# Input handed over twice, token-major and feature-major: the first layer starts without transposes

## The chip, the cores and the metric

One NeuronCore of a Trainium2 chip runs the whole program. Its engines are TensorE (PE, with its weight loads as PEld), VectorE (DVE), ScalarE (ACT), GpSimd (POOL) and SyncE (SP), which here only issues transfers. The metric is the device time of one launch in microseconds (us), lower is better.

## The reference, cut to what matters

Two decoder layers over 256 tokens of 1024 features, all in float32. Each layer:

```
u = RMSNorm(h) * g_mix
proj = u @ w_in                     # index q/k/w and ka, va | qb | kb | vb | qa | gate_a | gate_b
mixer A: index scores -> the 64 best causal keys of each query -> attention over them (8 heads)
mixer B: two causal softmax maps for each of 4 heads, their difference weighted by lambda, RMSNorm
h += (sigmoid(gate_a) * (A @ w_branch_a) + sigmoid(gate_b) * (B @ w_branch_b)) @ w_out
h += convffn(RMSNorm(h));  h += sigmoid(RMSNorm(h) @ w_ple_gate) * (p[i] @ w_ple_proj)
```

The norm divides each token by the root of the mean of its squares. This factor 1/rms is one number per token, so the kernel multiplies it onto the projection's result instead of onto its input.

## The kernel before, in words

**Products.** Every operand is split into two fp32r parts, hi and lo (`HL` for activations, `wh` and `wl` for weights), and a product is three matmuls: hi with `wh`, hi with `wl`, lo with `wh` (L335 to L337). In `gemm_a` (L318) a projection of 512 columns has 8 steps, one for each 128 features (k). A step does the three matmuls for both halves of the tokens, so 6 matmuls, and a projection has 48. The result stands in two of four rotating accumulators (`ps_acc`, L117), which `evict` empties after the last step. The activation must stand feature-major (features on the partitions), so token-major `h` is transposed by PE first (`split_T2`, L286: transposes at L298, hi part on ACT at L301, lo part on DVE at L302).

**Weights.** They come in chunks of 512 KB (128 x 1024), each good for two steps. `dma_next` issues the load on SP's queue in order into one of five raw buffers; the split of a chunk is one ACT copy (`wh`, L159) and one DVE subtraction (`wl`, L166), and the subtraction frees the raw buffer and issues the next load. The first two chunks are split by halves (`split_piece`, L172).

**Side work and its order.** The order of every engine's instructions is written out when the program is made. Class `Side` (L59) keeps planned clocks for PE, DVE and ACT. Attention, rope, the selection of keys and the like are threads of stages. After every two steps `tick` (L82) lets each thread emit its next stage if three things hold: its last stage is planned to be done, the planned DVE clock is at most 3.5 us (`LIMIT_US`) ahead of the planned PE clock, and no more than 2 us of side work went onto PE in this tick. After it, one more chunk is split as a rule. Lower priority numbers go first: rows and heads 0, mixers 1, selection of keys (`select_side`) 2. Where a result is needed, `until` (L101) emits side stages alone, with no product between them, until its flag is set: for mixer B before its branch product (L747), for mixer A before its own (L754).

**The start (layer 0).** SP loads `h` in two pieces of 256 columns with chunks 0 and 1 behind each, then the other 512 columns, chunks 2 and 3, the tables, chunk 4 and on. PE does seven warm-up products, transposes k = 0 and 1, two more warm-ups, transposes k = 2 and 3, and begins the index projection (452 columns, chunks 0 to 3). Before its third step `mid` transposes k = 4 to 7; before its seventh step `norm` sums the squares of `h` on ACT (`sq_half`), forms 1/rms on POOL (`rstd`) and starts the thread `th` that makes the rope tables; the index result is evicted with 1/rms as its scale, and its rows (`index_side`) are spawned. Then come the projections qb, kb, vb, qa (8 steps each), four gate products, branch B (two products of 4 steps), branch A (the same) and the rest of the layer.

Of the kernel before, what the change touches and what calls it, by code (L numbers as in the profile page):

```python
# [38 lines left out]
N_WARM = (7, 2)  # L39
# [9 lines left out]
T_AT = 1  # L49
# [10 lines left out]
class Side:  # L60
    """Side work emitted in stages between groups of the main products.

    A thread is a generator; after each stage it yields estimates of the time (us) the stage takes
    on the tensor, vector and scalar engines. A stage is emitted once the tensor engine is expected
    to reach it no earlier than the thread's previous stage ends, so that it is not held up."""
# [43 lines left out]
def decoder_kernel(ctx: ExitStack, tc: tile.TileContext, x, pT, ws, fc, tb, gf, rope, out):  # L109
# [26 lines left out]
    def warm_up(n):  # L136
        """Products without use that keep the tensor engine's clock up while the first loads run."""
        for _ in range(n):
            nc.tensor.matmul(wps, warm[:, :P], warm[:, :512], start=True, stop=True)
    warm_up(N_WARM[0])  # L140

# [1 line left out]
    raws, parts = {}, {}  # L143
    nx = {"dma": 0, "hi": 0, "lo": 0, "cur": 0, "held": 0}

    def dma_next(step=CW):
        l, c = divmod(nx["dma"], NCHUNK)
        raw = wpool.tile([P, CW], F32, name="raw", bufs=RAWS)
        for a in range(0, CW, step):
            nc.sync.dma_start(raw[:, a:a + step], ws[l, c][:, a:a + step])  # L150
        raws[nx["dma"]] = raw
        nx["dma"] += 1

# [18 lines left out]
    def split_piece(a, n):  # L172
        """Columns a to a + n of the next chunk."""
        if a == 0:
            parts[nx["hi"]] = (wpool.tile([P, CW], F32R, name="wh", bufs=SPLITS),
                               wpool.tile([P, CW], F32R, name="wl", bufs=SPLITS))
        raw, (wh, wl) = raws[nx["hi"]], parts[nx["hi"]]
        nc.scalar.activation(wh[:, a:a + n], raw[:, a:a + n], AF.Copy)
        nc.vector.tensor_sub(wl[:, a:a + n], raw[:, a:a + n], wh[:, a:a + n].bitcast(F32))
        if a + n == CW:  # L180
            raws.pop(nx["lo"])
            nx["hi"] += 1
            nx["lo"] += 1
            dma_next()

    def prepare(n_lo, n_hi):
        """Have the parts of the chunks before n_lo and n_hi emitted."""
        while nx["lo"] < min(n_lo, NALL):
            if nx["hi"] == nx["lo"]:
                split_hi()  # L190
            split_lo()
        while nx["hi"] < min(n_hi, NALL):
            split_hi()
# [22 lines left out]

    for c in range(2):
        nc.sync.dma_start(h[:, :, c * 256:(c + 1) * 256], xv[:, :, c * 256:(c + 1) * 256])
        dma_next(512)
    nc.sync.dma_start(h[:, :, HALF[1]], xv[:, :, HALF[1]])  # L220
# [8 lines left out]

    for c in range(RAWS - 2):  # L230
        dma_next()
        if c == T_AT:
            load_tables()
# [19 lines left out]
    def sq_half(ss, hf, tiles=(0, 1)):  # L253
        """ss[hf][:, i] = sum of h^2 / D over half of the columns."""
        for i in tiles:
            junk = sm.tile([P, 512], F32, name="junk", **T2)
            nc.scalar.activation(junk, h[:, i, HALF[hf]], AF.Square, scale=1.0 / 32, accum_out=ss[hf][:, i:i + 1])  # L257
# [15 lines left out]
    class HL:  # L273
        """fp32r parts hi + lo of [128, 8, 256] operands, stored by halves of the k index."""
# [11 lines left out]
    def split_T2(srcs, hf, k0, scale, x, between=None):  # L286
        """Parts (columns k0, k0 + 1 of half hf of x) of the transpose of two [128, 512] tiles; the scale is
        one for all k or a function of k."""
        hi, lo = x.h[hf][:, k0:k0 + 2, :], x.l[hf][:, k0:k0 + 2, :]
        n = 1 if callable(scale) else 2  # L290
        pts = []
        for a in range(0, 2, n):
            pt = ps_tp.tile([P, 2, L], F32, name="tp")[:, :n, :]
            pts.append(pt)
            for j in range(n):
                for i in range(2):
                    c = (k0 + a + j) * P
                    nc.tensor.transpose(pt[:, j, i * P:(i + 1) * P], srcs[i][:, c:c + P], ident)  # L298
        for a in range(0, 2, n):
            s = scale if n == 2 else scale(4 * hf + k0 + a)  # L300
            nc.scalar.activation(hi[:, a:a + n, :], pts[a], AF.Copy, scale=s)  # L301
            nc.vector.scalar_tensor_tensor(lo[:, a:a + n, :], pts[a], s, hi[:, a:a + n, :].bitcast(F32),  # L302
                                           op0=ALU.mult, op1=ALU.subtract)
            if between:
                between(a)
# [12 lines left out]
    def gemm_a(x, ks, weights, n, evict, mid=None, before_evict=None, outer=0):  # L318
        """Token-major product: evict(i, psum) for the two token tiles; mid[s]() before step s. The last
        `outer` k go through the first token tile, then through the second."""  # L320
# [27 lines left out]
    def tables(l, t):  # L348
        """Tables of the layer: rope with gains, lambda, sub-norm gain."""
# [30 lines left out]
    def rope_rows(dst, src, n, tabs, i, dup=False):  # L380
        """dst, src [128, n, 64]"""
        m1 = sm.tile([P, 8, 64], F32, name="m1", **T2)[:, :n, :]
        m2 = sm.tile([P, 8, 64], F32, name="m2", **T2)[:, :n, :]
        tA = tabs[:, i, 0, :].unsqueeze(1)
        nc.vector.tensor_mul(m1, src, tA.broadcast_to([P, n, 64]))
        for a, b in ((0, 32), (32, 0)):
            tB = tabs[:, i, 1, a:a + 32].unsqueeze(1)
            nc.vector.tensor_mul(m2[:, :, a:a + 32], src[:, :, b:b + 32], tB.broadcast_to([P, n, 32]))
        if dup:
            nc.vector.tensor_add(dst, m1.broadcast_to([P, 2, 64]), m2.broadcast_to([P, 2, 64]))  # L390
        else:
            nc.vector.tensor_add(dst, m1, m2)
# [8 lines left out]
    def transposed(srcs, nb, dst):  # L401
        """dst [128, nb, 256] from two token-major [128, nb*128] tiles."""
# [9 lines left out]
    def stacked(q3):  # L412
        """fp32r [128 t, n, 2, 64] of [128 t, n, 64]: the two parts of each head side by side."""
# [6 lines left out]
    def transposed_parts(srcs, dsts):  # L420
        """[128, n, 256] (in tiles of 4) from two stacked [128 t, n, 128]."""
# [12 lines left out]
    def begin(k0):  # L434
        split_T2([h[:, i, HALF[0]] for i in range(2)], 0, k0, lambda k: g0[:, k:k + 1], u,
                 lambda j: split_piece(j * 512, 512))
    begin(0)
    warm_up(N_WARM[1])
    begin(2)
    env, th = tables(0, tbs[0])  # L440

    for l in range(DEPTH):
# [7 lines left out]
        st = {}  # L450

        def mid():
            for k0 in (0, 2):
                split_T2([h[:, i, HALF[1]] for i in range(2)], 1, k0, lambda k: g_mix[:, k:k + 1], u)
                if l == 0:
                    prepare(3 + k0 // 2, 3 + k0 // 2)
            if l:
                norm()
# [3 lines left out]

        def norm():
            if l == 0:
                side.dve += BEHIND_US
                side.spawn(th, 0)
                sq_half(ss, 0)
# [5 lines left out]
        def project(c0, n, name, mid=None):  # L473
            pr = [sm.tile([P, 512], F32, name=f"pr{name}", **T2) for _ in range(2)]

            def ev(i, acc):
                nc.scalar.activation(pr[i][:, :n], acc[:, :n], AF.Copy, scale=st["rs"][:, i:i + 1])
# [85 lines left out]
        def heads_side(pr, nm, is_q):  # L563
            """Rope of eight heads, transposed; 1/rms beside the queries, in the keys."""
# [28 lines left out]
        def maps(qn, product, i, hq, mk):  # L593
            """Four masked score maps, exp'd, [128 t, 4, S]; head 4 hq + 2 m + r."""
# [21 lines left out]
        def ptrans(src, nh, i):  # L616
            """[128 s, nh * blocks, 128 t] of [128 t, nh, S]."""
# [103 lines left out]

# [1 line left out]
        pi = project(C_IDX, N_IDX, "i", {MID_N: mid} if l else {MID_0: mid, 6: norm, 7: more})  # L723
        side.spawn(index_side(pi), 0)
        side.spawn(heads_side(project(C_QB, 512, "q"), "qb", True), 0)
# [50 lines left out]
        def ev_n(i, acc):  # L776
            """Second half of the columns of a token tile, then its norm for the ffn."""
# [175 lines left out]
def _layout(np, inp):  # L953
    """Inputs as the launch reads them: rows and columns moved, nothing computed."""
# [47 lines left out]
    return {"x": inp["x"][0], "pT": pT, "ws": ws, "fc": np.stack(fc), "tb": np.stack(tb), "gf": np.stack(gf), "rope": rope}  # L1002
# [19 lines left out]
```

## Time and profile before

| | |
|---|---|
| Time, median of 3 runs | 800.34 us (798.68 to 802.0) |
| Span of the profiled execution | 798.6 us, 0.1 us below the fastest of the three runs |
| Busy share of the span | PE 99%, PEld 86%, DVE 76%, ACT 60%, POOL 8% |
| Chain that ended last | PE 93%, DVE 2%, POOL, ACT, DMA and issue 1% each |
| Granted TensorE clock | full in the records from early in the span to its end |
| Index, qb, kb projections begin (PE) | 7.91, 18.84, 29.7 us |

The span runs from the first to the last instruction. The profile gives no separate device time for the profiled execution, so its own time is taken as its span.

### The profile page before, as it was taken

To read this page: it belongs to the slowest core of one execution; us is meant where nothing else is said; L and a number is where in the kernel's file an instruction comes from. 1 tells how busy PE (TensorE), PEld (TensorE's weight loads), DVE (VectorE), ACT (ScalarE), POOL (GpSimd) and SP (SyncE) were. 2 spreads that over 40 slices of the span, in tenths; PEclk is the share of its full clock that TensorE was granted. 3 is DMA by queue.
4 is the path that set the end of the run, shared out by engine and by line. 5 is a ranking of instruction groups with operands and counts; after the bars stand their busy time and mean duration, and the time that the engine had idled before them with its cause. 6 is when DMAs were issued, how large, how long until landed. Compare 5 with 4: busy or idle time off the path is not lost.

```text
span 798.6 us, 12832 instructions
## 1 busy us (share of the span) xinstructions
PE 789.2 (99%) x4801; PEld 690.7 (86%) x4801; DVE 605.8 (76%) x1084; ACT 477.8 (60%) x843; POOL 63.2 (8%) x87
## 2 busy tenths in 40 slices
PE   8999999999999999999999999999999999999997
PEld 6877887788999999888888778878899999998887
DVE  6988986777888888754687889778688888884643
ACT  6767658366666666553566486575476666663541
POOL 0250300010000000000123212000100000000000
PEclk9999999999999999999999999999999999999999
DMA  8644463574555555656464335445555555567421
GB/s 324 205 158 134 132 211 106 172 235 135 185 185 185 184 185 180 228 172 225 133 201 162 125 121 188 154 132 191 190 160 184 185 185 186 184 190 259 162 102 53
DMA packets 40334, 139.58 MB, mean 175 GB/s; under 512 B 4560, under 2 KB 5968, under 8 KB 40272
## 3 DMA queue, kind: packets, MB, share of 16 engines
q1 hardware_dynamic: 39408, 136.91, 52.0%
q10 hardware_dynamic: 864, 1.84, 0.7%
q8 instruction: 38, 0.62, 0.3%
q14 instruction: 24, 0.20, 0.1%
HBM read 137.69 MB, written 1.05 MB: 174 GB/s over the span
## 4 chain that ended last, share of the span: by engine, by line
PE 93%; DVE 2%; POOL 1%; ACT 1%; DMA 1%; issue 1%; SPq 0%; DVEq 0%; ACTq 0%; POOLq 0%
PE acc L335 12%; PE acc L337 12%; PE acc L336 12%; PE tp L828 11%; PE tp L827 11%; PE tp L829 11%; PE acc L883 5%; PE acc L881 5%; PE acc L882 5%; PE tp L298 2%; PE tp L626 1%; PE tp L634 1%; POOL rq L251 1%; PE tp L705 1%; PE tp L639 1%; PE tp L605 1%
## 5 line engine op out<-in xcount | busy, mean ns | idle before, releaser
L166 DVE TENSOR_TENSOR wl<-raw,wh 128x1024 fp32r<-128x1024 f32 x254 | 306.2, 1219 | 25.9 <-ACT wh L159 25.4
L159 ACT ACTIVATE wh<-raw 128x1024 fp32r<-128x1024 f32 x254 | 264.7, 1057 | 38.8 <-PE acc L883 30.1
L828 PE MATMUL tp<-ul,wh 128*128 128x256 f32 x704 | 199.4, 283 | 0.0
L827 PE MATMUL tp<-uh,wh 128*128 128x256 f32 x704 | 199.4, 283 | 0.0
L829 PE MATMUL tp<-uh,wl 128*128 128x256 f32 x704 | 199.2, 283 | 0.0
L828 PEld LDWEIGHTS tp<-ul,wh 128*128 128x128 f32 x704 | 135.1, 192 | 0.1
L827 PEld LDWEIGHTS tp<-uh,wh 128*128 128x128 f32 x704 | 135.1, 192 | 0.0
L829 PEld LDWEIGHTS tp<-uh,wl 128*128 128x128 f32 x704 | 135.1, 192 | 0.0
L335 PE MATMUL acc<-wh,uh 128*128 128x512 f32 (+1 forms) x336 | 133.7, 398 | 0.0
L337 PE MATMUL acc<-wh,ul 128*128 128x512 f32 (+1 forms) x336 | 130.6, 389 | 0.0
L336 PE MATMUL acc<-wl,uh 128*128 128x512 f32 (+1 forms) x336 | 130.3, 388 | 0.0
L834 DVE SCALAR_TENSOR_TENSOR cv<-tp,fc,cv 128x255 f32<-128x255 f32 (+1 forms) x176 | 84.9, 483 | 40.2 <-ACT cv L832 37.0
L832 ACT ACTIVATE cv<-tp,fc 128x256 f32<-128x256 f32 x88 | 49.6, 564 | 90.0 <-PE tp L829 90.0
L337 PEld LDWEIGHTS acc<-wh,ul 128*128 128x128 f32 x336 | 63.1, 188 | 12.9
L335 PEld LDWEIGHTS acc<-wh,uh 128*128 128x128 f32 x336 | 63.2, 188 | 11.8 <-issue 0.3
L336 PEld LDWEIGHTS acc<-wl,uh 128*128 128x128 f32 x336 | 63.2, 188 | 11.6 <-DVE wl L166 0.2
L881 PE MATMUL acc<-wh,gh 128*128 128x512 f32 x176 | 68.9, 391 | 0.0
L883 PE MATMUL acc<-wh,gl 128*128 128x512 f32 x176 | 68.5, 389 | 0.0
L882 PE MATMUL acc<-wl,gh 128*128 128x512 f32 x176 | 68.5, 389 | 0.0
L265 POOL TENSOR_SCALAR sst<-ss 128x2 f32<-128x2 f32 (+1 forms) x8 | 5.6, 699 | 513.0 <-ACT junk L257 512.9
L611 ACT ACTIVATE pe<-tp,nb,rq 128x256 f32<-128x256 f32 (+1 forms) x64 | 31.8, 523 | 17.4 <-DVE nb L608 13.6
L883 PEld LDWEIGHTS acc<-wh,gl 128*128 128x128 f32 x176 | 33.0, 188 | 6.9
(185 smaller groups left out, 1018.9 us busy)
## 6 DMA issues: line engine op xcount, KB each, us to landing
raw<-ws SPq DMA_DIRECT2D x254, 512.0 KB, 3.4
raw<-ws SPq DMA_DIRECT2D x4, 256.0 KB, 5.0
gb<-gf ACTq DMA_DIRECT2D x2, 512.0 KB, 4.5
h<-x SPq DMA_DIRECT2D x2, 256.0 KB, 4.1
h<-x SPq DMA_DIRECT2D x1, 512.0 KB, 6.4
px<-pT ACTq DMA_DIRECT2D x2, 256.0 KB, 2.6
out<-h SPq DMA_DIRECT2D x2, 256.0 KB, 2.0
out<-h SPq DMA_DIRECT2D x4, 128.0 KB, 1.7
```

Of the source, the lines that this page charges most:

```text
L159: nc.scalar.activation(wh, raw, AF.Copy)
L166: nc.vector.tensor_sub(wl, raw, wh.bitcast(F32))
L335: nc.tensor.matmul(o, a, wh, start=q == 0, stop=False)
L336: nc.tensor.matmul(o, a, wl, start=False, stop=False)
L337: nc.tensor.matmul(o, b, wh, start=False, stop=q == nk - 1)
L827: nc.tensor.matmul(pu, wh[:, k, :], u.hi(k), start=k == 0, stop=False)
L828: nc.tensor.matmul(pu, wh[:, k, :], u.lo(k), start=False, stop=False)
L829: nc.tensor.matmul(pu, wl[:, k, :], u.hi(k), start=False, stop=k == KD - 1)
L834: nc.vector.scalar_tensor_tensor(c[:, sh:], pu[:, :L - sh], w[:, 2 - sh:3 - sh], c[:, sh:], op0=ALU.mult, op1=ALU.add)
L881: nc.tensor.matmul(acc[i], a, wh, start=k == 0, stop=False)
L882: nc.tensor.matmul(acc[i], a, wl, start=False, stop=False)
L883: nc.tensor.matmul(acc[i], b, wh, start=False, stop=k == NF - 1)
```

## The change

`x` is also passed as `xT`, feature-major [128, 8, 256]. The start of layer 0 loads `xT` in the places where it loaded `h` and splits it directly (`split_x`, from SBUF, without PE). `h` is loaded later, in two halves of 512 KB, behind chunks 5 and 6; the tables come behind chunk 7 instead of behind chunk 3. The squares and 1/rms move into the next projection (qb), with the eviction of the index result, the start of `th` and the spawn of `index_side`. The warm-up is ten products in one piece. Layer 1 is unchanged. Comments were dropped.

```diff
-N_WARM = (7, 2)
+N_WARM = 10
-T_AT = 1
+H_AT = (6, 7)
+T_AT = 8
...
         nx["dma"] += 1
+        if nx["dma"] in late:
+            late.pop(nx["dma"])()
...
+    xts = [blk.tile([P, 4, L], F32, tag="blk", name="xt") for _ in range(2)]
     for c in range(2):
-        nc.sync.dma_start(h[:, :, c * 256:(c + 1) * 256], xv[:, :, c * 256:(c + 1) * 256])
+        nc.sync.dma_start(xts[0][:, 2 * c:2 * c + 2, :], xT[:, 2 * c:2 * c + 2, :])
         dma_next(512)
-    nc.sync.dma_start(h[:, :, HALF[1]], xv[:, :, HALF[1]])
+    nc.sync.dma_start(xts[1], xT[:, 4:8, :])
...
+    def load_h(hf):
+        nc.sync.dma_start(h[:, :, HALF[hf]], xv[:, :, HALF[hf]])
+    late.update({H_AT[0]: lambda: load_h(0), H_AT[1]: lambda: load_h(1), T_AT: load_tables})
     for c in range(RAWS - 2):
         dma_next()
-        if c == T_AT:
-            load_tables()
...
-    begin(0)
-    warm_up(N_WARM[1])
-    begin(2)
+    def split_x(k):
+        src, s = xts[k // 4][:, k % 4, :], g0[:, k:k + 1]
+        nc.scalar.activation(u.hi(k), src, AF.Copy, scale=s)
+        nc.vector.scalar_tensor_tensor(u.lo(k), src, s, u.hi(k).bitcast(F32), op0=ALU.mult, op1=ALU.subtract)
+    for k in range(4):
+        split_x(k)
+        split_piece(k % 2 * 512, 512)
...
         def mid():
             for k0 in (0, 2):
-                split_T2([h[:, i, HALF[1]] for i in range(2)], 1, k0, lambda k: g_mix[:, k:k + 1], u)
-                if l == 0:
+                if l:
+                    split_T2([h[:, i, HALF[1]] for i in range(2)], 1, k0, lambda k: g_mix[:, k:k + 1], u)
+                else:
+                    split_x(4 + k0)
+                    split_x(5 + k0)
                     prepare(3 + k0 // 2, 3 + k0 // 2)
...
+        held = []
+        def flush():
+            assert not late
+            side.dve += BEHIND_US
+            side.spawn(th, 0)
+            for f in held:
+                f()
+            side.spawn(index_side(pi), 0)
         def norm():
-            if l == 0:
-                side.dve += BEHIND_US
-                side.spawn(th, 0)
-                sq_half(ss, 0)
             sq_half(ss, 1)
...
-        pi = project(C_IDX, N_IDX, "i", {MID_N: mid} if l else {MID_0: mid, 6: norm, 7: more})
-        side.spawn(index_side(pi), 0)
-        side.spawn(heads_side(project(C_QB, 512, "q"), "qb", True), 0)
+        pi = project(C_IDX, N_IDX, "i", {MID_N: mid} if l else {MID_0: mid, 7: more}, hold=l == 0)
+        if l:
+            side.spawn(index_side(pi), 0)
+            qb_mid = None
+        else:
+            qb_mid = {3: lambda: sq_half(ss, 0), 5: norm, 7: flush}
+        side.spawn(heads_side(project(C_QB, 512, "q", qb_mid), "qb", True), 0)
```

With `hold`, `project` puts the two evictions into `held`; `flush` emits them before the last step of qb.

## Rows read from the trace of the kernel before

**Rows 1.** The page: span, and busy time, share and instructions of each engine.
```profile
span 798.6 us, 12832 instructions
PE 789.2 (99%) x4801; PEld 690.7 (86%) x4801; DVE 605.8 (76%) x1084; ACT 477.8 (60%) x843; POOL 63.2 (8%) x87
```
**Rows 2.** PE's waits, first 200 us: waiter, releaser, total us, times, longest.
```profile
PE tp L298 <- DMA h<-x: 1.2, 1, 1.2
PE tp L639 <- ACT pe L611: 0.6, 1, 0.6
PE tp L408 <- DVE qr L577: 0.5, 1, 0.5
```
**Rows 3.** The chain that ended last, first 20 us: start, length, what.
```profile
2.20 5.24 DMA h<-x
7.49 0.66 PE tp L298 x4
10.62 0.87 PE tp L298 x8
...
19.00 0.23 PE acc L335
```
**Rows 4.** Timeline of the start: start, length, instruction [idle before, releaser].
```profile
1.44 3.17 PE L139 MATMUL acc<-warm 128*128 128x512 bf16 x7 [1.44 <-DVE mhalf L130]
...
11.60 1.06 ACT L159 ACTIVATE wh<-raw 128x1024 fp32r<-128x1024 f32 x1
...
12.70 1.23 DVE L166 TENSOR_TENSOR wl<-raw,wh 128x1024 fp32r<-128x1024 f32 x1 [0.44 <-ACT wh L159]
...
13.98 0.19 PEld L336 LDWEIGHTS acc<-wl,uh 128*128 128x128 f32 x1 [0.18 <-DVE wl L166]
...
15.60 1.06 ACT L159 ACTIVATE wh<-raw 128x1024 fp32r<-128x1024 f32 x1 [1.26 <-DMA raw<-ws]
...
21.83 0.61 POOL L266 TENSOR_TENSOR sst<-sst,ss 128x2 f32<-128x2 f32 x1 [1.09 <-ACT junk L257]
22.51 0.73 POOL L267 TENSOR_TENSOR rstd<-sst,mhalf 128x2 f32<-128x2 f32 x1
...
23.27 1.17 ACT L477 ACTIVATE pri<-acc,rstd 128x452 f32<-128x452 f32 x2 [0.65 <-POOL rstd L267]
```
**Rows 5.** DMA, first 24 us, in 40 slices of 0.6 us.
```profile
GB/s 0 0 2 79 342 314 311 239 239 248 230 358 382 386 403 434 416 403 418 379 376 372 402 410 396 416 403 423 396 416 403 416 280 389 348 266 307 287 294 382
```
**Rows 6.** Issue and landing of chunk 2, then of chunk 9.
```profile
L150 SPq DMA_DIRECT2D raw<-ws x1: 465/465/465, 4.1 to 4.1; - x1
DMA to landing us min/median/max: 7.2/7.2/7.2
...
L150 SPq DMA_DIRECT2D raw<-ws x1: 328/328/328, 17.9 to 17.9; - x1
DMA to landing us min/median/max: 4.0/4.0/4.0
```
**Rows 7.** Single lines, layer 0: duration ns min/median/max, first and last start.
```profile
L257 ACT ACTIVATE junk<-h x4: 614/616/617, 19.1 to 21.0; 128x512 f32<-128x512 f32 x4
L509 PE MATMUL tp<-ident,kk x4: 271/272/273, 37.9 to 38.2; 128*128 128x128 f32 x4
L639 PE MATMUL tp<-kT,qT x32: 221/280/366, 115.9 to 124.3; 128*128 128x256 f32 x16, 128*128 128x128 f32 x16
L705 PE MATMUL tp<-pt,va x24: 379/379/430, 131.1 to 144.4; 128*64 128x256 f32 x24
```
**Rows 8.** Busy time in stretches: length; PE, PEld, DVE, ACT, POOL; clock; DMA.
```profile
18.84:29.72 10.88, 10.88 (x49) 9.01 (x48) 9.87 (x33) 8.49 (x18) 3.17 (x6) 1.00 0.66 227
72.00:112.00 40.00, 40.00 (x207) 33.78 (x207) 39.10 (x110) 26.72 (x55) 7.84 (x12) 1.00 0.48 157
```
**Rows 9.** Timeline of mixer A: a transposed map on PE and its copies on ACT.
```profile
127.39 1.03 PE L626 MATMUL tp<-ident,pe 128*128 128x128 f32 x8
128.77 1.15 ACT L627 ACTIVATE pt<-tp 128x512 f32<-128x512 f32 x2
```

More of the change, by code (lines that the diff above doesn't have):

```diff
@@ L108, in decoder_kernel @@
 @with_exitstack
-def decoder_kernel(ctx: ExitStack, tc: tile.TileContext, x, pT, ws, fc, tb, gf, rope, out):
+def decoder_kernel(ctx: ExitStack, tc: tile.TileContext, x, xT, pT, ws, fc, tb, gf, rope, out):
     nc = tc.nc
@@ L139, in warm_up @@
             nc.tensor.matmul(wps, warm[:, :P], warm[:, :512], start=True, stop=True)
-    warm_up(N_WARM[0])
-    raws, parts = {}, {}
+    warm_up(N_WARM)
+    raws, parts, late = {}, {}, {}
     nx = {"dma": 0, "hi": 0, "lo": 0, "cur": 0, "held": 0}
@@ L432, in decoder_kernel @@
     g0 = fcs[0][:, 0:8]
-    def begin(k0):
-        split_T2([h[:, i, HALF[0]] for i in range(2)], 0, k0, lambda k: g0[:, k:k + 1], u,
-                 lambda j: split_piece(j * 512, 512))
-    begin(0)
-    warm_up(N_WARM[1])
-    begin(2)
+    def split_x(k):
[5 more added lines that the diff above has]
+        split_piece(k % 2 * 512, 512)
     env, th = tables(0, tbs[0])
@@ L471, in norm, with project, f @@
             nc.gpsimd.tensor_scalar(st["rsh"], st["rs"], 0.5, None, op0=ALU.mult)
-        def project(c0, n, name, mid=None):
+        def project(c0, n, name, mid=None, hold=False):
             pr = [sm.tile([P, 512], F32, name=f"pr{name}", **T2) for _ in range(2)]
             def ev(i, acc):
-                nc.scalar.activation(pr[i][:, :n], acc[:, :n], AF.Copy, scale=st["rs"][:, i:i + 1])
+                def f():
+                    nc.scalar.activation(pr[i][:, :n], acc[:, :n], AF.Copy, scale=st["rs"][:, i:i + 1])
+                if hold:
+                    held.append(f)
+                else:
+                    f()
             gemm_a(u, range(KD), stream(l, c0, n), n, ev, mid)
@@ L720, in o_side @@
             flags.add("ob")
-        pi = project(C_IDX, N_IDX, "i", {MID_N: mid} if l else {MID_0: mid, 6: norm, 7: more})
-        side.spawn(index_side(pi), 0)
-        side.spawn(heads_side(project(C_QB, 512, "q"), "qb", True), 0)
+        pi = project(C_IDX, N_IDX, "i", {MID_N: mid} if l else {MID_0: mid, 7: more}, hold=l == 0)
+        if l:
+            side.spawn(index_side(pi), 0)
+            qb_mid = None
+        else:
+            qb_mid = {3: lambda: sq_half(ss, 0), 5: norm, 7: flush}
+        side.spawn(heads_side(project(C_QB, 512, "q", qb_mid), "qb", True), 0)
         side.spawn(heads_side(project(C_KB, 512, "q"), "kb", False), 0)
@@ L1001, in _layout @@
     rope = rope.reshape(2, P, 2, 64).transpose(1, 0, 2, 3)
-    return {"x": inp["x"][0], "pT": pT, "ws": ws, "fc": np.stack(fc), "tb": np.stack(tb), "gf": np.stack(gf), "rope": rope}
+    x = inp["x"][0]
+    xT = x.T.reshape(KD, P, L).transpose(1, 0, 2)
+    return {"x": x, "xT": xT, "pT": pT, "ws": ws, "fc": np.stack(fc), "tb": np.stack(tb), "gf": np.stack(gf), "rope": rope}
 def kernel(**inputs):
```

## The prediction

> **What bounds the kernel now.** I read the page first: PE is busy for 789.2 of 798.6 us [rows 1], so time is won only where PE idles or does work that can go. Then PE's waits, and for layer 0 they are short: 1.2 us for the second piece of `h`, 0.6 us in mixer A, 0.5 us for a key row of kb [rows 2]. The chain of the first 20 us shows what stands ahead of the products: the load to 7.44, four transposes, and later eight transposes of 0.87 us [rows 3]. The timeline shows something less visible: after the eight transposes PE caught up with the split of chunk 2, and its fourth-next matmul waited 0.18 us for that chunk's `wl` [rows 4]. So at 14 us the limit was already the load of the weights: ACT stood idle 1.26 us for chunk 4 [rows 4], and DMA moved about 400 GB/s from 7 to 19 us without a gap [rows 5].
>
> **Part 1: the transposes and the start.** Sixteen transposes go; eight stand on the chain with 0.87 us, the others ahead of the first product [rows 3]. `split_x` costs ACT and DVE the same count of operations as before (eight each); their source is now SBUF, which no row shows for this form; the nearest, a 128x512 square from SBUF at 616 ns [rows 7], bounds it from above, and a gain of 0.1 us each from below; I take no change.
> PE can begin when the first half of chunk 0 is in, after ten warm-ups at 3.17/7 = 0.45 us from 1.44 [rows 4], so at about 5.9 instead of 7.91. A step is 10.88/8 = 1.36 us in a projection of 512 columns [rows 8], about 1.24 us with 452. Four steps would end at 10.9 to 11.7. The fifth needs chunk 2, and the bytes ahead of chunk 2 are what they were: 1 MB of input, chunks 0 and 1. It landed at 4.1 + 7.2 = 11.3 [rows 6]. From there ACT takes 1.06 and DVE 1.23 us [rows 4], with the steps between some 13.5 us, against 14.0 now. So nearly all that the transposes give back turns into a wait for chunk 2: index ends at 18.4 instead of 18.84, a gain of 0.45. Rows of 1 KB become 2 KB: if that removed the dip to 239 GB/s between 4.2 and 6.6 us [rows 5], chunk 2 would come 2.4 x (1 - 239/400) = 1.0 us sooner; from below nothing. I take 0.1 (the rate rises while such rows are still moving, so they are not the plain cause).
>
> **Part 2: `h` a second time.** It adds 1.05 MB to a stretch in which DMA is full: at 400 GB/s 2.6 us for every chunk behind it. The queue past which it is moved is SP's, in order: chunk 5, half of `h`, chunk 6, the other half, chunk 7, tables (0.57 MB, no new bytes), chunk 8. Chunk 9 landed at 17.9 + 4.0 = 21.9 [rows 6]; it will at about 24.4. For qb and kb themselves this hides: chunk 8 is split by about 25.5, and kb wants it at 29.3.
>
> **Part 3: the held eviction.** In ACT's order the tick after qb's second step puts the copy of chunk 9, then come two squares, the copy of chunk 10, two squares, then 1/rms on POOL, then the eviction. From 24.4: copy 1.06, two squares 2 x 0.62, copy 1.06, two squares 1.24 [rows 4, 7], so 29.0; from the last square to the eviction now passes about 1.6 us (21.7 to 23.27) [rows 4], so 30.6; the first tile's eviction is half of 1.17 [rows 4], 31.2. qb ends at 18.4 + 10.88 = 29.3. kb's first matmul writes the accumulators that the index result still holds (four rotate, qb has the other two). PE waits 1.9 us there, a wait that the trace does not have; behind it stand all of kb, and behind ACT's own waits the splits of chunks 10 and 11, which kb does not need until later. Bounds: 0 (chunk 9 by 22.5) to 3 us (chunk 10 as late again as in the present slices under 300 GB/s [rows 5]). kb starts at 31.2 against 29.72.
> The Trainium skill (Perfetto Trace Analysis, Optimizing Tensor Performance) tells one to rotate matmul groups through different PSUM banks so that one group's evacuation overlaps the next group's matmuls. The present trace does that; the held eviction gives it up for two of four banks. By the rule alone there is a loss and no size.
> The Trainium skill (DMA: Bandwidth & Descriptors, Where 436 GB/s comes from) puts the limit of HBM loads near 358 GB/s a core; the slices here are 372 to 434 from 7 to 19 us, so the measurement decides. By the page the second `h` would cost 2.9 us and kb would start 0.3 later.
>
> **Part 4: side work begins later.** `th` and `index_side` start after qb, 9 steps later. DVE is the reason that this is not free: from 72 to 112 us it is busy 39.1 of 40 us [rows 8], so what it misses early comes out at the end. I worked the planned clocks of `tick` by hand: a tick adds 2.6 us to PE, a split 1.12 to DVE, and a stage its own estimates. Numbering pairs of steps from the start (index 1 to 4, qb 5 to 8, kb 9 to 12, vb, qa, gates 21 to 36, branch B 37 to 40, branch A 41 to 44), the same ledger for the kernel before puts the index transposes after pair 11, mixer B's maps after 17, mixer A's after 33 and its last product after 39. The trace agrees: L509 at 37.9, L639 from 115.9, L705 to 144.4 [rows 7], each at that count of main matmuls.
> For the changed kernel: after pair 8 the clocks are PE 20.8 and DVE 21.3 (splits 19.3, `BEHIND_US` 2); `th` and the first index row bring DVE to 25.9, the split to 27.0, over the limit of 24.3 + 2.6 at the next tick. Then: qb rows after 10 and 13, second index row 11, index transposes 15, kb rows 15 and 17, index scores 17 and 18, mixer B's maps 19 and 20, qa rows 21 and 23, the four rounds of selection 28, 30, 32, 34, the mask 36, mixer A's maps 38 and 39, its first transposed maps 40. The deficit grows from 2 pairs at mixer B to 5 at mixer A, since qa's rows have priority over the selection. The flag for mixer B still comes in time (35 of 36). Mixer A does not: its product stages are left for `until`, ahead of branch A, with no main product between.
> Price: PE's work there is the same; what is added is what the main products hide now. The first transposed maps end 0.8 us after 127.39, their copies on ACT at 129.9, because ACT comes from the exponentials and a split [rows 9]: 1.7 us idle. Then the other three transposes run in one go, two more waits of 0.2 and 0.4 us for copies and for the last hi part. Sum 2.3 us. Bounds: 0 if mixer A keeps its place, 4.6 if its maps come one pair later still (all copies then wait uncovered).
> Against it, kb's wait gives DVE a lead of 1.9 us in the rows behind it, which covers the 0.5 us wait for the key row [rows 2]: -0.5. The 0.6 us in mixer A stays; it is the exponentials that hold the banks.
>
> **Sum.** -0.45 + 1.9 - 0.5 + 2.3 = +3.25 us. The profiled span of 798.6 becomes 801.9; the median of the runs is 1.7 above the span, and I add to it: 800.34 + 3.25 = 803.6 us.
> Clock: before the change PE idled 1.2 us ahead of the second piece of `h` [rows 2], and the stretch after it is at the full level, 2.4 GHz [rows 8]. The two new gaps are 1.5 to 1.9 us; I cost them at nothing. The warm-ups stand 0.45 us apart at the lower level, 1.2 GHz, against 0.23 for a product of the same columns later [rows 3, 4]: each microsecond at the lower level would cost half of one, and a fall as long as the start, from 1.44 to 7.91 at most, 3.2 us.
>
> **Rivals.** (1) Mixer A keeps its place, because the ledger is two or more pairs off: 803.6 - 2.3 = 801.3. For it: the ledger for before was up to two pairs off at the o transposes. Against: the deficit is five.
> (2) Mixer A one pair later still, or one fall of the clock: 803.6 + 2.3 = 805.9. For it: the same uncertainty with the other sign.
> (3) Faster: the rate of the loads. If they ran at the best slice, 434 GB/s [rows 5], from the first byte at 2.2, chunk 2 (2.62 MB) is in at 8.2, index runs without a wait from 5.9 to 15.9, qb to 26.8; chunk 9 (7.92 MB) at 20.4, kb at 27.2 instead of 29.72: -2.5 - 0.5 + 2.3 = -0.7, 799.6. It decides from a kb start before 27.9, which needs 419 GB/s sustained. Against it: no slice before 7 us is over 358, and the mean after is 400.
>
> **How the numbers follow.** Forecast 803.6, 47%; (1) 25%; (2) 20%; (3) 8%. The range 799.4 to 806.9 leaves out half of (3) and a third of (2). A measurement of this kernel can tell 0.5% (4 us) from no change, so 796.3 to 804.3 counts as the same. Slower: 0.3 of the forecast, most of (2), so 0.32. Faster by so much needs (3) and mixer A in place together: 0.06. Same: 0.62.
>
> **What would show it.** In the changed profile: first product at 5.3 to 5.9; PE idle near 12 to 13.5, ended by chunk 2's `wl`; kb's first product idle for about 2 us near 29 to 31, ended by the index eviction or 1/rms; mask and mixer A's maps four to five pairs later, and PE idle between its products, ended by the copies `pt`. Without a wait at kb's start, part 3 is wrong; with mixer A's last product ahead of branch A's tick, part 4 is wrong; and if chunk 2 lands before 10, part 1.

## The result, and the profile of the changed kernel

The changed kernel takes 805.72 us (median of 4 runs, 805.52 to 806.71), the kernel before 800.22 us beside it (798.68 to 802.0): a ratio of 1.0077, 95% interval 1.0061 to 1.0092. It is slower, by 5.5 us in these runs; in the runs of the experiments, where the kernel before was timed 42 times in two series, its medians are 799.29 and 799.38, and the changed kernel, timed again in the second series, has 806.07. So the loss is 6.7 us in that series, and 6.4 us with the 805.72 above. The forecast was 803.6, 3.25 us slower.

The page of the changed kernel, span and busy time of the engines, against [rows 1]:

```profile
span 803.8 us, 12805 instructions
PE 789.1 (98%) x4786; PEld 690.1 (86%) x4786; DVE 606.0 (75%) x1084; ACT 478.5 (60%) x843; POOL 63.2 (8%) x87
```

PE lost instructions (15 fewer matmuls) and is busy for the same time to 0.1 us; the span grew by 5.2 us. All of this growth is therefore idle time of PE, and the view that answers the question is PE's waits. Here are those of the first 210 us, against [rows 2] (waiter, releaser, total us, times, longest):

```profile
PE acc L340 <- ACT pri L496: 1.6, 1, 1.6
PE tp L431 <- ACT pt L650: 1.6, 1, 1.6
PE tp L728 <- ACT pt L650: 1.5, 1, 1.5
...
PE tp L413 <- DVE qr L600: 1.0, 1, 1.0
PE acc L341 <- DVE wl L169: 0.8, 1, 0.8
PE tp L649 <- DVE ol L733: 0.6, 1, 0.6
PE tp L662 <- ACT pe L634: 0.5, 1, 0.5
PE tp L431 <- DVE ob L698: 0.5, 1, 0.5
PE tp L685 <- ACT qT L432: 0.2, 1, 0.2
PE acc L340 <- ACT wh L162: 0.2, 1, 0.2
```

Before there were three rows with 2.3 us; now there are ten with 8.5 us (the wait ahead of the warm-ups and one of 0.2 us in a later stage are the same in both and not counted). From the top: kb's first matmul waits for the held eviction; qa's transposes (L431), with 1.6 and 0.5 us and 0.2 us behind them (L685); mixer A's products (L728) and its last transposed maps (L649); the key row of kb (L413), twice what it was; the fifth step of index (L341, L340) in place of the transposes of `h`; and the exponentials of mixer A as before.

The start in PE's, ACT's and DVE's timeline, against [rows 3, 4] (start, length, instruction, idle before and releaser):

```profile
5.53 0.75 PE L340 MATMUL acc<-wh,uh 128*128 128x452 f32 x1
...
10.94 1.06 ACT L162 ACTIVATE wh<-raw 128x1024 fp32r<-128x1024 f32 x1 [0.52 <-DMA raw<-ws]
...
12.04 1.22 DVE L169 TENSOR_TENSOR wl<-raw,wh 128x1024 fp32r<-128x1024 f32 x1 [1.09 <-ACT wh L162]
...
13.31 0.47 PE L341 MATMUL acc<-wl,uh 128*128 128x452 f32 x1 [0.78 <-DVE wl L169]
```

The first product stands 2.4 us earlier (5.53 against 7.91), and half-way through index PE waits for chunk 2: its copy begins at 10.94, when the load is in, then it is subtracted, and its `wl` is used at 13.31.

ACT on the way to the held eviction, and what waits for it on PE:

```profile
24.38 1.06 ACT L162 ACTIVATE wh<-raw 128x1024 fp32r<-128x1024 f32 x1 [0.22 <-DMA raw<-ws]
...
26.57 1.05 ACT L162 ACTIVATE wh<-raw 128x1024 fp32r<-128x1024 f32 x1
27.52 0.61 ACT L262 ACTIVATE junk<-h 128x512 f32<-128x512 f32 x1
...
28.75 1.04 ACT L162 ACTIVATE wh<-raw 128x1024 fp32r<-128x1024 f32 x1
...
30.17 1.17 ACT L496 ACTIVATE pri<-acc,rstd 128x452 f32<-128x452 f32 x2 [0.38 <-POOL rstd L272]
```

```profile
30.86 0.50 PE L340 MATMUL acc<-wh,uh 128*128 128x512 f32 x1 [1.62 <-ACT pri L496]
```

The copy at 24.38 was released by chunk 9's DMA; from there ACT runs copies and squares without a break until 1/rms is needed, and the eviction starts at 30.17. qb had ended at 29.1.

The two late places in PE's timeline, qa's transposes and the end of mixer A, against [rows 9]:

```profile
93.26 0.46 PE L431 MATMUL tp<-identr,qs 128*128 128x128 f32 x4
95.30 0.54 PE L431 MATMUL tp<-identr,qs 128*128 128x128 f32 x4 [1.58 <-ACT pt L650]
...
145.61 1.03 PE L649 MATMUL tp<-ident,pe 128*128 128x128 f32 x8
148.18 1.08 PE L728 MATMUL tp<-pt,va 128*64 128x256 f32 x8 [1.54 <-ACT pt L650]
...
151.28 0.66 PE L649 MATMUL tp<-ident,pe 128*128 128x128 f32 x4 [0.56 <-DVE ol L733]
```

In the second, no main product stands between the transposed maps and the products on them; the next main matmul, branch A's, comes at 153.9. In the first, PE waits for copies of mixer B's transposed maps, which PE had done by 90.4, ahead of a main pair. ACT's timeline tells why they came so late:

```profile
91.61 1.05 ACT L162 ACTIVATE wh<-raw 128x1024 fp32r<-128x1024 f32 x1
92.56 1.24 ACT L770 ACTIVATE tg<-acc,rsh 128x512 f32<-128x512 f32 x2
93.70 1.05 ACT L162 ACTIVATE wh<-raw 128x1024 fp32r<-128x1024 f32 x1
94.65 1.35 ACT L650 ACTIVATE pt<-tp 128x512 f32<-128x512 f32 x3
```

A split, an eviction and another split stand ahead of the copies, and the second four of qa's transposes stand behind them.

**Where the 6.4 us come in.** The transposes `tp` that close the same 45th pair of steps start at 162.17 before and at 168.59 after: the whole loss, 6.4 us, is there by a fifth of the span. Of it, kb starts 1.14 us later (30.86 against 29.72), the key row costs 0.5 more, qa's transposes 1.6 + 0.5 + 0.2 = 2.3, the end of mixer A 1.5 + 0.6 = 2.1; the exponentials 0.1 less. That makes 5.9 of 6.4; the remaining 0.5 us are not placed. The profiled spans differ by 5.2 only, because the profiled execution of the kernel before has a wait of its own in layer 1. PE's waits behind 210 us, kernel before, and the two POOL instructions that the waiting row needs, before and then after:

```profile
PE tp L408 <- DVE qr L577: 1.0, 1, 1.0
```

```profile
448.72 1.24 POOL L250 TENSOR_SCALAR pw<-hss 128x8 f32<-128x8 f32 x1 [5.11 <-DVE hss L398]
450.04 2.15 POOL L251 TENSOR_TENSOR rq<-pw,mhalf 128x8 f32<-128x8 f32 x1
```

```profile
455.13 0.56 POOL L255 TENSOR_SCALAR pw<-hss 128x8 f32<-128x8 f32 x1 [5.11 <-DVE hss L403]
455.78 1.69 POOL L256 TENSOR_TENSOR rq<-pw,mhalf 128x8 f32<-128x8 f32 x1
```

The same two instructions take 3.39 us in the one and 2.25 us in the other. In all nine other traces they take 0.56 or 0.57 and 1.69 us, and none has the wait, also where layer 1 is the code of before (`e2_hold_only`). In every execution that has both numbers the device time is 1.7 to 1.9 us above the span (805.56 against 803.8 for the changed kernel). So the profiled execution of before, with a span of 798.6, took about 800.34 and was not the fastest of its runs: it is 1 us above the medians of the 42. The 1.0 us belongs to that execution and is no gain of the change; why POOL was slower there, the traces do not show.

### The profile page after: what moved, and what is told of

It is laid out like the page before. It is cut to its first block, busy times and chain, and to the rows that moved or that the text cites. A ratio compares the mean times of both kernels' runs of the same rounds, so it can differ in the third digit from the quotient of the medians.

```text
span 803.8 us, 12805 instructions
## 1 busy us (share of the span) xinstructions
PE 789.1 (98%) x4786; PEld 690.1 (86%) x4786; DVE 606.0 (75%) x1084; ACT 478.5 (60%) x843; POOL 63.2 (8%) x87
## 3 DMA queue, kind: packets, MB, share of 16 engines
HBM read 138.74 MB, written 1.05 MB: 174 GB/s over the span
## 4 chain that ended last, share of the span: by engine, by line
PE 87%; DVE 4%; ACT 4%; DMA 2%; issue 1%; POOL 1%; ACTq 0%; POOLq 0%; DVEq 0%
PE acc L340 11%; PE acc L342 11%; PE acc L341 11%; PE tp L855 11%; PE tp L856 11%; PE tp L854 11%; PE acc L908 5%; PE acc L910 5%; PE acc L909 5%; DMA raw<-ws 2%; ACT pe L634 1%; DVE wl L169 1%; PE tp L303 1%; ACT wh L162 1%; PE tp L657 1%
## 5 line engine op out<-in xcount | busy, mean ns | idle before, releaser
L340 PE MATMUL acc<-wh,uh 128*128 128x512 f32 (+1 forms) x336 | 133.8, 398 | 1.9 <-ACT pri L496 1.6
L341 PE MATMUL acc<-wl,uh 128*128 128x512 f32 (+1 forms) x336 | 130.7, 389 | 0.8 <-DVE wl L169 0.8
L340 PEld LDWEIGHTS acc<-wh,uh 128*128 128x128 f32 x336 | 63.4, 189 | 14.9 <-ACT pri L496 2.0
L341 PEld LDWEIGHTS acc<-wl,uh 128*128 128x128 f32 x336 | 63.4, 189 | 13.2 <-DVE wl L169 1.1
```

Source lines behind the costliest of these rows:

```text
L340: nc.tensor.matmul(o, a, wh, start=q == 0, stop=False)
L341: nc.tensor.matmul(o, a, wl, start=False, stop=False)
```

## The experiments

**Theory A:** the order costs the time. Holding the eviction starts `th` and `index_side` nine steps later, and DVE, which has no slack up to mixer A, delivers late to places without cover. **Theory B:** the second load of `h` does, by its 1.05 MB in a full stretch of DMA. The first two runs make the change's two halves apart.

**`e1_xt_plain`**: xT and the late loads stay; squares, 1/rms, `th`, the eviction and `index_side` go back into index.

```
+ (in norm)  if l == 0:
+                side.dve += BEHIND_US
+                side.spawn(th, 0)
+                sq_half(ss, 0)
- pi = project(C_IDX, N_IDX, "i", {MID_N: mid} if l else {MID_0: mid, 7: more}, hold=l == 0)
+ pi = project(C_IDX, N_IDX, "i", {MID_N: mid} if l else {MID_0: mid, 6: norm, 7: more})
+ side.spawn(index_side(pi), 0); qb_mid = None
```

> Keeps xT, the second load of h behind chunks 5 and 6 and the tables behind chunk 7; undoes the hold: squares, 1/rms, eviction, rope tables and index rows stand where they stood before the change. Theory A (the loss is the late side work in the written-out order, plus the wait at kb's start): index ends at 18.2 us, no wait at kb's start, mixer A's maps back after pair 33; about 799.5 us, at most 800.5 if the rows run later because h and the tables land later. Theory B (the loss is the second load of h, 1 MB that delays every weight chunk behind it): most of the 5.5 us stays, 803 to 806 us.

Measured: 798.64 us, 0.9991 of before [0.9982, 1.0]: 0.65 us less, at the edge of what these runs can tell. Of PE's waits those of the start stay, and at the key row it is the 0.5 us of [rows 2] again:

```profile
PE acc L341 <- DVE wl L169: 0.8, 1, 0.8
...
PE acc L340 <- ACT wh L162: 0.5, 1, 0.5
PE tp L413 <- DVE qr L604: 0.5, 1, 0.5
```

The second load of `h` is in this kernel, and no loss is: by itself it does not cost the time, and theory B falls. What it costs together with the hold is below.

**`e2_hold_only`**: the kernel before, with the hold, its flush and the moved squares alone.

```
+ held = []
+ def flush(): (as in the change: BEHIND_US, th, the held evictions, index_side)
- (in norm, for l == 0: BEHIND_US, th and sq_half(ss, 0) go)
+ (project takes hold, as in the change)
- pi = project(C_IDX, N_IDX, "i", {MID_N: mid} if l else {MID_0: mid, 6: norm, 7: more})
+ pi = project(C_IDX, N_IDX, "i", {MID_N: mid} if l else {MID_0: mid, 7: more}, hold=l == 0)
...
+ qb_mid = None if l else {3: lambda: sq_half(ss, 0), 5: norm, 7: flush}
```

> The kernel before with the hold alone: token-major start with its transposes, no xT, loads in their old order; squares at qb's steps 3 and 5, index eviction, rope tables and index rows after qb. Theory A: no wait at kb's start, since chunk 9 lands at 21.9 and the eviction is done at about 28.8, ahead of qb's end at 29.7; mixer A's maps after pair 38 as in the changed kernel, and the same waits at qa's transposes (about 2.3 us) and in mixer A (about 2.3 us); 804 us, between 803 and 805. Theory B: without the second load nothing is lost, 800 to 801 us.

Measured: 804.44 us, 1.007 [1.0057, 1.0082]. The same waits as in the changed kernel, without the one at kb's start:

```profile
PE tp L426 <- ACT pt L637: 1.6, 1, 1.6
PE tp L715 <- ACT pt L637: 1.5, 1, 1.5
...
PE tp L408 <- DVE qr L587: 1.0, 1, 1.0
```

L426, L715 and L408 are L431, L728 and L413 of the changed kernel. So the order alone costs 804.44 - 799.29 = 5.1 us, with `h` loaded once and the transposes in place: theory A holds.

The four cells together: before 799.29, xT alone -0.65, hold alone +5.15, both +6.4 (805.72, timed in another series; +6.7 beside its own). The sum of the halves is +4.5. The 1.9 us above it fit the wait at kb's start, 1.6 us in the trace, which only the hold and the second `h` together make; the next run tests this.

**`e4_tables_11`**: the changed kernel with `T_AT = 8` replaced by `T_AT = 11`, so that the tables stand behind chunk 10 on SP's queue instead of ahead of chunk 8.

> The changed kernel with one number changed: the tables (0.57 MB) are loaded behind chunk 10 instead of chunk 7, so chunks 8 to 10 land 1.4 us sooner. ACT's queue ahead of the held eviction then starts at 21.7 instead of 23.1. If the wait at kb's start is the landing of chunks 8 and 9, as forecast, it shrinks from 1.8 to about 0.4 us and the time by up to 1.4 us, to 804.3. If a wait there is paid back by the rows behind it, as the forecast had it (a lead for DVE), the waits behind grow and the time stays at 805.7.

Measured: 804.05 us, 1.0066 [1.0052, 1.008]; 1.7 us below the 805.72 of the changed kernel. At kb's start PE waits 0.2 us:

```profile
PE acc L340 <- ACT pri L496: 0.2, 1, 0.2
```

Chunk 9's copy begins at 22.44 instead of 24.38, and the eviction at 28.52 instead of 30.17. The waits at L431, L728 and L413 are what they were. So the wait at kb's start is made by bytes ahead of chunks 8 to 10, it is worth its full length at the end, and it is no part of the order's 5 us.

**`e7_flush_at_3`**: the changed kernel with the hold released earlier in qb.

```
- qb_mid = {3: lambda: sq_half(ss, 0), 5: norm, 7: flush}
+ qb_mid = {0: lambda: sq_half(ss, 0), 1: norm, 3: flush}
```

> The changed kernel with the squares at qb's steps 0 and 1 and the flush (eviction, rope tables, index rows) ahead of step 3 instead of step 7. In the written-out order the index transposes stand after pair 11 (changed kernel 15, before 11), mixer B's maps after 18 (19, 17), mixer A's after 33 to 35 (38, 33), its last product after 40. Theory A, order: the waits at qa's transposes (2.3 us) and in mixer A before its branch product (2.3 us) go, the wait at kb's start goes too (eviction at about 28 us); against it the data of the rows is still late, so up to 2 us of waits appear at the index transposes after pair 11: 800 to 802 us. Theory B, the second load of h: within 1 us of the changed kernel.

Measured: 800.21 us, 1.0008 [0.9999, 1.0017]; 5.9 us below the changed kernel in the same runs (806.07). Mixer A's maps stand behind pairs 33 to 35 again, and its last product behind pair 40. PE's waits:

```profile
PE acc L341 <- DVE wl L169: 1.4, 2, 0.8
...
PE acc L340 <- ACT wh L181: 0.7, 1, 0.7
PE tp L532 <- ACT kk L522: 0.5, 1, 0.5
...
PE tp L413 <- DVE qr L600: 0.4, 1, 0.4
```

None of the waits at qa's transposes, at the end of mixer A or at kb's start is left. By the four cells above, an estimated 1.9 of the 5.9 us are kb's start, and some 4 the order. The held eviction itself, in `e2_hold_only` and then here:

```profile
27.63 1.17 ACT L483 ACTIVATE pri<-acc,rstd 128x452 f32<-128x452 f32 x2 [0.37 <-POOL rstd L267]
```

```profile
28.20 1.17 ACT L496 ACTIVATE pri<-acc,rstd 128x452 f32<-128x452 f32 x2 [0.63 <-POOL rstd L272]
```

The index result is ready later here than in `e2_hold_only`, which loses 5.1 us. So the loss does not come from the time at which the data is ready, but from the place in the written-out order at which the side work of layer 0 may begin: four steps, 5.4 us of PE's time at 1.36 a step, decide it. They do not give back everything: this kernel is still 0.8 us above before, and `e1_xt_plain`, in the other series, 0.65 us below it.

**`e8_select_first`**: the changed kernel with the selection of layer 0 ranked with the head rows, so that mixer A's maps come at their old place.

```
- side.spawn(select_side(rels, wvs), P_TOPK)
+ side.spawn(select_side(rels, wvs), P_TOPK if l else 0)
```

> The changed kernel with the selection of keys at priority 0 in layer 0, so that it goes ahead of mixer B and of qa's rows. Mixer A's maps then stand after pairs 33 to 35 and its products ahead of branch B; mixer B's last stages fall into the loop ahead of branch B instead, after pair 36, with no main product between. If the loss is a fixed deficit of DVE work that has to come out somewhere, the waits move from mixer A to the place after pair 36 and the time stays within 1.5 us of the changed kernel. If it was the place of the selection alone (the late mask), 2 to 4 us are won, 801.5 to 803.

Measured: 811.37 us, 1.015 [1.0134, 1.0165]. Both expectations missed. The maps do come behind pairs 33 to 35, but PE's waits are more and longer (the row of `wh` is the start):

```profile
PE tp L662 <- ACT pe L634: 2.5, 1, 2.5
PE tp L649 <- DVE pe L718: 1.7, 1, 1.7
...
PE acc L340 <- ACT wh L162: 1.6, 1, 1.6
...
PE tp L649 <- DVE wl L169: 1.4, 1, 1.4
```

The end of mixer B and mixer A now fall together, ahead of branch B, and both want DVE and ACT there. This ranking did not remove the late work; what is done first makes something else late, here at a dearer place. Not all of the 5.3 us over the changed kernel in the same series (806.07) is the ranking, though: the 1.6 us on `wh` are the wait for chunk 2, whose copy begins at 12.20 instead of 10.94. qb starts at 19.42 against 17.99 in `c0_after`, and up to there the two programs are the same. So 1.4 us of this execution's loss are late loads; whether the other three had them is not known.

**`e5_chunk2_first`**: `e1_xt_plain` with chunk 2 loaded ahead of xT's second half and prepared ahead of its split. It asks what the start gains when index does not wait.

```
+ dma_next()
  nc.sync.dma_start(xts[1], xT[:, 4:8, :])
- for c in range(RAWS - 2):
+ for c in range(RAWS - 3):
...
+ prepare(3 + k0 // 2, 3 + k0 // 2)     (moved ahead of the two splits of xT)
```

> e1 with chunk 2 loaded ahead of the second half of xT and split ahead of k = 4 and 5. If the load and split of chunk 2 is what holds PE at the fifth step (0.2 + 0.8 us of waits in the changed kernel), these waits go, index ends at 17.2 instead of 18.2 us and the time is 1.0 us below e1's, about 798.5. If another load takes its place (k = 4 and 5 of xT land when chunk 2 did), below 0.3 us of difference to e1.

Measured: 798.51 us, 0.9992 [0.9983, 1.0001]: nothing against `e1_xt_plain` (798.64). Yet the waits of the fifth step are gone: PE runs without a listed wait from 5.54 on, and the last product of the 11th pair starts at 35.95, 1.2 us before the 37.14 of `e1_xt_plain`. It is given back at kb's key row, whose wait grew from 0.5 to 1.5 us. DVE's timeline has a likely reason, a rope table that came late:

```profile
PE tp L414 <- DVE qr L605: 1.5, 1, 1.5
```

```profile
21.04 0.29 DVE L369 TENSOR_TENSOR rt_ka<-rp,tbl 128x128 f32<-128x128 f32 x1 [1.48 <-DMA tbl<-tb]
```

**`e6_tables_early`**: `e5_chunk2_first` with the two tables that DVE wants first, `rp` and `tb[0]`, loaded ahead of chunk 7; the rest stays where it was.

```
+ def load_h1_tables():
+     load_h(1)
+     nc.sync.dma_start(rp, rope)
+     nc.sync.dma_start(tbs[0], tb[0])
- (the same two loads in load_tables)
- late.update({H_AT[0]: lambda: load_h(0), H_AT[1]: lambda: load_h(1), T_AT: load_tables})
+ late.update({H_AT[0]: lambda: load_h(0), H_AT[1]: load_h1_tables, T_AT: load_tables})
```

> e5 with the rope table and its gains loaded directly behind the second half of h, ahead of chunk 7, instead of behind chunk 7; chunk 7 lands 1.0 us later, which qb does not need before 23 us. In e5 DVE waited 1.5 us for these tables at 21 us and PE waited 1.5 us for the last key row of kb at 54 us. If the second wait is the first one carried along DVE's chain of rows, it shrinks to about 0.3 us and the time is 1 us below e5's: about 797.5. If the chain hangs on 1/rms and the index eviction instead, which now come up to 0.4 us later behind the copy of chunk 7, the time stays within 0.3 us of e5's 798.5.

Measured: 797.81 us, 0.9979 [0.997, 0.9988]. The wait at the key row falls from 1.5 to 0.8 us, and 0.7 us reach the end; 0.3 us of wait had been expected if the tables were its only reason, so they are about half of it, and the other half is open:

```profile
PE tp L416 <- DVE qr L607: 0.8, 1, 0.8
```

This version beats both kernels: 1.6 us below before, 8.3 us below the changed one. It shows what xT is worth here, once the hold is dropped and two loads are put nearer to where their users need them.

**`c0_after`**: the changed kernel itself, in one series with `e6_tables_early`, `e7_flush_at_3` and `e8_select_first`.

> The changed kernel itself, as the measure for the three beside it on the same chip: 804.5 to 806 us.

Measured: 806.07 us, 1.0085 [1.0071, 1.0098], just above what was expected. The waits are those of the first profile to 0.1 us, except at the start: the first product stands at 6.12 instead of 5.53, and qb still begins at 17.99 (18.17 there), because both wait 0.8 us for chunk 2's `wl`.

## Why the prediction was right or wrong

The direction was right, and so was the mechanism as far as it went; the size was not, since one wait had no term and another had the wrong sign: forecast +3.25 us, measured +6.4. The time of 805.7 lies in the range; most of the chance stood on less than 0.5%, and the loss is 0.77%. By its own steps:

- **The start: right.** Forecast 0.45 us, index ending at 18.4; qb's first product stands at 18.2. The first product at 5.53 was forecast for 5.3 to 5.9; the idle time in front of the fifth step, ended by `wl`, is there with 0.2 + 0.8 us. `e5_chunk2_first` shows that chunk 2 is the reason. What I did not see is that one more limit stands behind it, DVE's rows. One reading of [rows 4] was off: the weight load that waited 0.18 us is that of the fifth step's second product, the 14th behind the eight transposes and not the fourth; the conclusion, that chunk 2 is the limit, stands.
- **Chunk 9 and the wait at kb: right.** Landing forecast at about 24.4, the copy began at 24.38; eviction forecast at 30.6, measured 30.17; kb's start 31.2, measured 30.86. I had counted 1.45 us for this and the start together, and it was 1.14. `e4_tables_11` showed the cause and that nothing gives it back.
- **The order of the side work: right, pair for pair.** Index transposes behind pair 15, scores behind 17 and 18, mixer B's maps behind 19 and 20, mixer A's behind 38 and 39, its first transposed maps behind 40, the rest in `until`: all where the planned clocks had put them.
- **The end of mixer A: right.** 1.7 + 0.2 + 0.4 = 2.3 forecast, 1.5 + 0.6 = 2.1 measured.
- **"-0.5" at kb's key row: wrong, with the other sign.** I took the wait at kb's start as a lead for DVE that covers this row. The wait rose from 0.5 to 1.0 us. `e2_hold_only` has the same 1.0 us without any wait at kb's start, so the order made it and kb's wait gave no lead; `e7_flush_at_3` brings it to 0.4. A likely way, not tested by itself: `th` and `index_side` begin in that same late stretch and stand ahead of the row on DVE. An error of 1.0 us.
- **A missing term at qa's transposes: 2.3 us.** The prediction put mixer B two pairs late and gave no place to its transposed maps; in the traces the first of them stand behind pair 25, where they stood behind pair 20, while qa's transposes came one pair earlier, behind 26 instead of 27. There was no entry for what two pieces of side work do to each other when they come within a pair: mixer B's transposed maps wait in PSUM for ACT, which has a main pair's eviction and two splits ahead of their copies, and qa's transposes ask for the tiles one pair later; PE waits 1.6 us in front of the second four, then 0.5 and 0.2 us. I priced only the place where no main product stood between (`until`) and took every other place as covered. The numbers needed were in [rows 9], where a copy ends 1.5 us behind its transposes' last product; I used them for mixer A alone. No run moved this one meeting by itself: `e2_hold_only` has the same waits, `e7_flush_at_3` has none of them. This term and the last make up the miss: 1.0 + 2.3 = 3.3 us, where 6.4 - 3.25 = 3.15 were missing; the other terms are off by 0.3 us at most, and the 0.5 us that are not placed stand against them.
- **The profile's own time.** I took the sum from a profiled execution that itself carried 1.0 us which none of the nine other traces has. The forecast time was nearer to the measured one for that (2.1 us) than the forecast difference was (3.2 us).
- **Clock: right.** No fall with the new gaps: the mean granted clock is 0.999, and behind the gap at 30.86 the products stand 0.23 to 0.24 us apart, as before it.

The Trainium skill (Perfetto Trace Analysis, Optimizing Tensor Performance) advises rotating the matmul groups through different PSUM banks. The row at 30.86 agrees: with two of the four accumulators held, the next group waited 1.6 us for its evacuation. Here the size is set by when the loads let ACT get to the eviction: the wait is 0.2 us in `e4_tables_11`. By the limit that the Trainium skill states for HBM loads (DMA: Bandwidth & Descriptors, Where 436 GB/s comes from), about 358 GB/s a core, the prediction estimated kb's start at 31.5; it came at 30.86. The trace does not agree with the limit: the slices from 8 to 24 us moved 359 to 423 GB/s, so the measurement decides.

Of the rivals, mixer A one pair later still came nearest in time (805.9) and is not what happened: mixer A came where the forecast had it. The right time for another reason is no support for it.

## What to carry to other kernels

Taking work off a start buys only the distance to the next limit: here leaving out the transposes was worth 2.4 us at the first product and 0.65 us at the end, and 1.6 us once two loads were moved to suit their users. Where PE's instruction order is written out and PE is busy 98%, as here, work of the other engines that may start later came out at the far end, at the places without main products to cover it; price each place where late work meets other work for the same buffers, not only the last one. And a result that is left in its accumulator must be priced by who wants that accumulator next, and by the transfers that the engine must serve before it gets to the eviction.

## What the runs showed that I had not expected

The same two POOL instructions took 3.39 us in one execution and 2.25 or 2.26 us in nine others, at the same place of the program, and PE waited 1.0 us for it. One profiled execution can hold a wait that is not the kernel's; the other traces and the medians of many runs told it apart.

The first products of index are slow although the profile's granted clock is at full level there. Busy time by stretch, changed kernel (length; PE, PEld, DVE, ACT, POOL with counts; clock; DMA share; GB/s):

```profile
5.50:7.50 2.00, 2.00 (x5) 1.44 (x5) 1.99 (x4) 1.75 (x4) 0.00 (x0) 1.00 1.02 379
7.50:18.10 10.60, 9.59 (x45) 8.14 (x45) 8.10 (x12) 7.47 (x12) 0.00 (x0) 1.00 1.03 404
```

Five products fill 2.00 us at first, 0.40 each, and 45 fill 9.59 us later, 0.21 each. Part of the first is a wait that the view does not list: the second product, at 6.26, needs a `wl` that DVE had at 6.20. But the third to the fifth stand 0.38 and 0.35 us apart, and that differs from one execution to the next. The ten warm-ups, which are the same in all kernels with `xT`, in this execution and in that of `e7_flush_at_3`:

```profile
1.44 4.45 PE L140 MATMUL acc<-warm 128*128 128x512 bf16 x10 [1.44 <-DVE mhalf L131]
```

```profile
1.44 3.64 PE L140 MATMUL acc<-warm 128*128 128x512 bf16 x10 [1.44 <-DVE mhalf L131]
```

In the second the third to the fifth product stand 0.20 us apart, and in `c0_after` 0.20 and 0.21, another execution of the same kernel as the first. So PE's rate rises early in the span, about twofold, at a moment that is not fixed by the program, while the granted clock reads 1.00 from the first warm-up on. The ratio is about that of the two levels, 1.2 and 2.4 GHz; that it is the clock, no row here shows. It costs little in this kernel, since index waits for chunk 2 in either case.
